# Down projection by seven block products instead of eight, in two passes over its weights

## The chip, the cores and the metric

The kernel runs on one core of a Trainium2 chip. TensorE (PE) multiplies matrices, VectorE (DVE), ScalarE (ACT) and GpSimd (POOL) work element by element, and SyncE's queue (SP) issues the DMAs. The metric is the device time of one execution in microseconds (us). Before the change the median of 3 runs is 704.86 us (703.7 to 706.74).

## What is computed

One decoder layer over 512 tokens of width 1024: a token mixer (differential attention and sparse attention), then a gated feed-forward part. The change lies in the last matrix product of the second:

```python
h = rms_norm(x, ffn_pre_norm[l])
f = (jax.nn.silu(h @ w_gate[l]) * (h @ w_up[l])) @ w_down[l]
x = x + rms_norm(f, ffn_post_norm[l])
```

`w_gate` and `w_up` are 1024 x 2816, `w_down` is 2816 x 1024, all in float32.

## The kernel before

**Three products for one.** TensorE reads float32 data rounded to the type fp32r. To keep the precision, every operand is cut into a high part (a rounded copy, made by ScalarE) and a low part (the operand minus the high part, made by VectorE), and a product is the sum of three: high by high, low by high, high by low. `split_w` (L142 for the high part, L152 for the low one) does this to a loaded weight tile of 128 x 1024.

**Feed-forward stage.** The 2816 features are 22 tiles (NF) of 128. For each tile f, `ff_gate` (L1045) issues 48 matmuls of 128x128 by 128x512: 24 for the gate and 24 for the up product, over 8 tiles of the model width (hth and htl, 128 x 8 x 512 each) and the three parts. Then the silu chain runs: an exponential on ScalarE (L1049), and on VectorE an addition (L1050), a reciprocal (L1051) and two multiplications (L1052, L1053), of which the first needs the gate product and the second the up product, both in PSUM. The result, features by tokens, is cut into `ffh` (L1054, ScalarE) and `ffl` (L1055, VectorE). The first two tiles are done in two halves of 256 tokens, since the norms of the last tokens are not ready yet.

**Down projection.** The output is 512 tokens by 1024 columns and fills all eight banks of PSUM, as four token tiles of 128 (i) by two column halves of 512 (c). `down` (L1083) issues three matmuls for one (i, c) and one feature tile f: a 128 x 128 block of ffh or ffl is the stationary operand, and half a row of the weight tile, 128 x 512, the moving one. That is 24 matmuls of a feature tile and 528 in all. For the first 19 tiles f is the outer loop; the last three (LAST) are taken with i outermost, so that the token tiles end one after the other and the closing norm of one lies beside the matmuls of the next. The closing work on a token tile: the squares on ScalarE (L983), the reciprocal root of their mean on ScalarE and VectorE in steps of one column (L161 to L170), the gain (L1099), the scaling and residual sum (L1101) on VectorE, and two DMAs out (L1102).

**Buffers and order.** Weight tiles go through three buffers each for the raw tile, the high and the low part; a raw buffer is free once the low part is made (L137 issues the load), and a high or low buffer once the matmuls that read it are done. 36 slots of 128 x 512 (`sslot`) and two tiles of four such (`rope_tile`) hold ffh and ffl. The instructions of this part stand in the program in the order in which a reader would write them, and a planner orders them on each engine by a timeline of its own: at each step the instruction that stands first in the program among those that are ready by its reckoning. On the chip the engines then keep this order.

Of the kernel before, what the change touches and what calls it, by code (L numbers as in the profile page):

```python
# [17 lines left out]
P = 128  # L18
# [84 lines left out]
LAST = 3  # L103
# [12 lines left out]
def hybrid_block_kernel(  # L116
# [843 lines left out]

    g_post, g_pre = gain(0), gain(1)
# [13 lines left out]
    def row_rsqrt(src, tag):  # L975
        ss = cpool.tile([P, 1], F32, tag="ss" + tag, name="ss", bufs=2)
        act.activation(junk[tag], src, AF.Square, accum_out=ss)
        return rsqrt_of(ss, tag)

    def halves_rsqrt(src, tag, also):  # L980
        ss = cpool.tile([P, 2], F32, tag="ss" + tag, name="ss", bufs=2)
        for c in range(2):
            act.activation(junk["a"][:, :SEQ], src[c], AF.Square, accum_out=ss[:, c:c + 1])  # L983
            if c == 0:
                also(c)
        dve.tensor_tensor(ss[:, 0:1], ss[:, 0:1], ss[:, 1:2], OP.add)
        r = rsqrt_of(ss[:, 0:1], tag)
        also(1)
        return r

    CS = [slice(c * SEQ, (c + 1) * SEQ) for c in range(2)]
# [14 lines left out]
    def norm_pre(i):  # L1006
# [4 lines left out]
        for c in range(2):  # L1011
# [4 lines left out]
            d_h, d_l = (t[:, 4 * c:4 * c + 4, i * P:(i + 1) * P] for t in (hth, htl))  # L1016
# [3 lines left out]
    ffh, ffl, ffw = [None] * NF, [None] * NF, []  # L1020

    def ff_alloc(f):
        for j, (l, n) in enumerate(((ffh, "ffh"), (ffl, "ffl"))):
            k = 2 * f + j
            if k < NS:
                l[f] = sslot(f"{n}{f}")
            else:
                k -= NS
                if k % 4 == 0:
                    ffw.append(rope_tile())  # L1030
                l[f] = ffw[-1][:, k % 4]
# [6 lines left out]
    def ff_gate(f, ws, s0, s1, tag):  # L1038
        pts = wide(tag, "gu")
        for wi, w in enumerate(ws):  # L1040
            pt = pts[wi][:, s0:s1]
            n = 0
            for ww, hx in ((w[0], hth), (w[0], htl), (w[1], hth)):
                for k in range(NK):
                    pe.matmul(pt, w_col(ww, k), hx[:, k, s0:s1],  # L1045
                              start=(n == 0), stop=(n == 3 * NK - 1))
                    n += 1
        sl = A.tile([P, SEQ], F32, tag="silu", name="silu", bufs=2)[:, s0:s1]
# [4 lines left out]
        dve.tensor_tensor(sl, sl, pts[1][:, s0:s1], OP.mult)  # L1053
        act.activation(ffh[f][:, s0:s1], sl, AF.Copy)  # L1054
        dve.tensor_tensor(ffl[f][:, s0:s1], sl, f32(ffh[f][:, s0:s1]), OP.subtract)  # L1055
# [18 lines left out]
    for f in range(2, NF):  # L1074
        ff_alloc(f)
        ff_gate(f, ff_weights(f), 0, SEQ, ("gu", "o", "tr", "o")[f % 4])

    g_ffn = gain(2)
    acc = [wide(t, "acc") for t in ("tr", "o", "gu", "o")]

    def down(i, f, w, first, last, c):
        for n, (a, wi) in enumerate(((ffh, 0), (ffl, 0), (ffh, 1))):
            pe.matmul(acc[i][c], a[f][:, i * P:(i + 1) * P],  # L1083
                      w[wi][:, c * SEQ:(c + 1) * SEQ],
                      start=(first and n == 0), stop=(last and n == 2))

    for f in range(NF - LAST):
        w = split_w(load_w(wd[f]))
        for i in range(NT):
            for c in range(2):  # L1090
                down(i, f, w, f == 0, False, c)
    ws = [split_w(load_w(wd[f])) for f in range(NF - LAST, NF)]
    for i in range(NT):
        for c in range(2):
            for n, w in enumerate(ws):
                down(i, NF - LAST + n, w, False, n == LAST - 1, c)
        u, a, x_ = work("uf"), acc[i], halves(x2[i])
        uh = halves(u)
        r = halves_rsqrt(a, "c", lambda c: dve.tensor_tensor(uh[c], a[c], g_ffn[:, CS[c]], OP.mult))  # L1099
# [94 lines left out]
```

## Time and profile before

| | us |
|---|---|
| median of 3 runs | 704.86 |
| the profiled execution | 707.53 |
| its span, first to last instruction | 705.8 |
| TensorE busy in the span | 677.2 (96%) |
| VectorE busy | 458.5 (65%) |
| ScalarE busy | 291.9 (41%) |
| mean granted TensorE clock | 0.983 of full speed |

Busy times are sums over the span; the stages differ, and so the rows further down are taken stage by stage. The page's own time in matmuls counts overlapping, since matmuls are pipelined: the distance from the start of one to the start of the next is what one costs.

### The profile page before, as it was taken

Reading aid. Unit: us, or ns where it says so; the run is one execution under the profiler, and the core shown is the slowest. Engines: PE = TensorE matmul, PEld = TensorE weight load, DVE = VectorE, ACT = ScalarE, POOL = GpSimd, SP = SyncE. Lnnn points to the kernel's source line nnn. Section 1 sums busy time; section 2 is a strip of 40 time slices with the busy share of each in tenths; the row PEclk is TensorE's granted clock in tenths of the full one; section 3 lists DMA queues with packets and bytes.
Section 4 is the critical chain, followed back from the end, with each engine's and each line's share of the span. In section 5 each row is a group of like instructions: output and inputs, shape, how many; then the busy total and the mean of one; then the engine's idle time right before and its main releaser. Section 6 shows DMA issues by size and latency. Waiting matters only on the chain.

```text
span 705.8 us, 9312 instructions
## 1 busy us (share of the span) xinstructions
PE 677.2 (96%) x3539; PEld 565.6 (80%) x3539; DVE 458.5 (65%) x712; ACT 291.9 (41%) x605; POOL 100.5 (14%) x151
## 2 busy tenths in 40 slices
PE   8999999989999999998799999999999999999995
PEld 4988778879787888777788888888888888888884
DVE  4787795856788574679676776867768672222227
ACT  7333352654787776534323233232332321211113
POOL 0000000028777934500000000000000000000000
PEclk9999999999999999999899999999999999999998
DMA  8357857623432030270022332223322332222303
GB/s 314 130 146 258 295 180 277 215 104 92 162 106 91 16 106 1 90 268 31 1 90 90 96 113 90 90 89 96 114 90 90 92 108 99 90 90 94 114 2 119
DMA packets 25980, 83.62 MB, mean 118 GB/s; under 512 B 3408, under 2 KB 4304, under 8 KB 25040
## 3 DMA queue, kind: packets, MB, share of 16 engines
q1 hardware_dynamic: 25936, 83.03, 35.2%
q8 instruction: 28, 0.46, 0.3%
q14 instruction: 16, 0.13, 0.1%
HBM read 73.06 MB, written 9.96 MB: 118 GB/s over the span
## 4 chain that ended last, share of the span: by engine, by line
PE 76%; DVE 10%; DMA 5%; issue 4%; ACT 3%; SPq 1%; POOL 0%; DVEq 0%; ACTq 0%; POOLq 0%
PE gu L1045 33%; PE acc L1083 16%; PE fm L327 8%; PE mixp L817 3%; PE v L413 3%; PE tr L574 3%; PE avn L754 2%; PE sc L548 2%; PE sc L549 2%; DMA qk<-rope 2%; DVE p L619 1%; DMA wraw<-in_wf 1%; DMA gain<-in_grow 1%; DMA wraw<-in_wvg 1%; PE av L631 1%
## 5 line engine op out<-in xcount | busy, mean ns | idle before, releaser
L152 DVE TENSOR_TENSOR wlo<-wraw,whi 128x1024 fp32r<-128x1024 f32 x86 | 104.9, 1222 | 142.1 <-ACT whi L142 97.5
L142 ACT ACTIVATE whi<-wraw 128x1024 fp32r<-128x1024 f32 x88 | 92.9, 1060 | 213.1 <-PE gu L1045 89.1
L1045 PE MATMUL gu<-hth,whi 128*128 128x512 f32 (+1 forms) x352 | 85.7, 386 | 0.5 <-ACT hth L1017 0.5
L1045 PE MATMUL gu<-htl,whi 128*128 128x512 f32 (+1 forms) x352 | 84.8, 384 | 0.0
L1045 PE MATMUL gu<-hth,wlo 128*128 128x512 f32 (+1 forms) x352 | 84.3, 382 | 0.0
L1045 PEld LDWEIGHTS gu<-hth,whi 128*128 128x128 f32 x352 | 65.4, 193 | 14.0 <-ACT hth L1017 0.8
L1045 PEld LDWEIGHTS gu<-htl,whi 128*128 128x128 f32 x352 | 64.9, 191 | 13.0
L1045 PEld LDWEIGHTS gu<-hth,wlo 128*128 128x128 f32 x352 | 64.1, 188 | 13.1
L1051 DVE RECIPROCAL silu<-silu 128x512 f32<-128x512 f32 (+1 forms) x24 | 74.1, 3086 | 0.7
L554 DVE TENSOR_REDUCE nm<-sc 128x1 f32<-128x384 f32 (+3 forms) x96 | 44.4, 484 | 21.7 <-PE sc L550 21.3
L1083 PE MATMUL acc<-whi,ffl 128*128 128x512 f32 x144 | 56.0, 389 | 0.0
L1083 PE MATMUL acc<-wlo,ffh 128*128 128x512 f32 x144 | 56.0, 389 | 0.0
L1083 PE MATMUL acc<-whi,ffh 128*128 128x512 f32 x144 | 55.9, 389 | 0.0
L558 ACT ACTIVATE p<-sc,nm 128x384 f32<-128x384 f32 (+3 forms) x96 | 50.0, 528 | 10.6 <-DVE nm L554 9.1
L723 POOL TENSOR_TENSOR p<-p,l 128x128 f32<-128x128 f32 (+2 forms) x64 | 45.6, 740 | 1.3
L587 DVE TENSOR_TENSOR ptl<-tr,pth 128x384 fp32r<-128x384 f32 (+1 forms) x60 | 35.1, 595 | 12.2 <-ACT pth L584 11.9
L548 PE MATMUL sc<-kst,qst 128*128 128x128 f32 (+1 forms) x96 | 36.2, 379 | 4.9 <-ACT p L558 3.2
L327 PE MATMUL fm<-xh,whi 128*128 128x512 f32 x128 | 34.4, 404 | 3.1 <-ACT whi L142 3.1
L584 ACT ACTIVATE pth<-tr 128x384 fp32r<-128x384 f32 (+1 forms) x60 | 31.0, 527 | 9.1 <-PE tr L574 8.3
L1054 ACT ACTIVATE ffh<-silu 128x512 fp32r<-128x512 f32 (+1 forms) x20 | 11.8, 589 | 52.4 <-DVE silu L1053 52.4
L327 PE MATMUL fm<-xh,wlo 128*128 128x512 f32 x128 | 32.4, 391 | 0.0
L327 PE MATMUL fm<-xl,whi 128*128 128x512 f32 x128 | 32.1, 390 | 0.0
(234 smaller groups left out, 1219.2 us busy)
## 6 DMA issues: line engine op xcount, KB each, us to landing
wraw<-in_wg SPq DMA_DIRECT2D x22, 512.0 KB, 3.3
wraw<-in_wu SPq DMA_DIRECT2D x22, 512.0 KB, 3.3
wraw<-in_wd SPq DMA_DIRECT2D x22, 512.0 KB, 3.3
wraw<-in_wf SPq DMA_DIRECT2D x16, 512.0 KB, 4.9
qk<-rope SPq DMA_DIRECT2D x7, 1024.0 KB, 4.7
kst<-qk SPq DMA_DIRECT2D x24, 256.0 KB, 3.6
qst<-qk SPq DMA_DIRECT2D x16, 256.0 KB, 2.7
wraw<-in_wo SPq DMA_DIRECT2D x8, 512.0 KB, 3.6
```

The source lines that it names most:

```text
L142: act.activation(dst, src, AF.Copy)
L152: (lo_eng or dve).tensor_tensor(lo[:, :w], raw[:, :w], f32(hi[:, :w]), OP.subtract)
L327: pe.matmul(pt, w[:, k * P:(k + 1) * P], xx[k], start=(n == 0), stop=(n == 3 * NK - 1))
L548: pe.matmul(sv[i], lhs, kk[:, 0, :w], start=True, stop=False)
L554: dve.tensor_reduce(nm[i], sv[i], AX.X, OP.max, negate=True)
L558: act.activation(pp[i], sv[i], AF.Exp, bias=nm[i], accum_out=hs["l"][:, row, i:i + 1])
L584: act.activation(part(u, 0), tv[u], AF.Copy)
L587: dve.tensor_tensor(part(u, 1), tv[u], f32(part(u, 0)), OP.subtract)
L723: pool.tensor_tensor(p, p, hs["l"][:, 1 + br, i:i + 1].to_broadcast(list(p.shape)), OP.mult)
L1045: pe.matmul(pt, w_col(ww, k), hx[:, k, s0:s1], start=(n == 0), stop=(n == 3 * NK - 1))
L1051: dve.reciprocal(sl, sl)
L1083: pe.matmul(acc[i][c], a[f][:, i * P:(i + 1) * P], w[wi][:, c * SEQ:(c + 1) * SEQ], start=(first and n == 0), stop=(last and n == 2))
```

## The change

Feature tiles are taken in pairs (2p, 2p+1) for p = 0 to 8. With tokens in two halves (256 each) and output columns in two halves (512 each), a pair's part of the output is a 2 x 2 by 2 x 2 product of blocks, and Winograd's form of Strassen's method makes it of seven block products, with sums of blocks on both sides made by VectorE. A block product is six matmuls of the shape used before: two token tiles by three parts. The last four feature tiles (18 to 21) go through `down` as before.

Since four results and the sums of products need more than eight banks, there are two passes. Pass A makes products 1, 5, 6 and 7 of all nine pairs in four accumulators of two banks. Products 1, 5 and 7 are then copied to SBUF, and `join` adds them up with product 6, still in PSUM, in pass B after pair 5. Pass B makes the other three products of each pair in the accumulators that have come free, and the last four tiles add to the same banks; the closing work adds PSUM to the parts in SBUF. Of the even weight tile the whole is loaded in pass A, of the odd one a half in pass A and the whole in pass B.

In the gate stage the cut of the 18 tiles into ffh and ffl is replaced by `pair_sums`, once a pair. The chain of the last tile (21) stands in the program behind the preparation of pairs 0 and 1. hth and htl become four tiles of 128 x 4 x 512, whose buffers are used again in the down projection.

```diff
-LAST = 3
+LAST = 4
+NPAIR = 9
+KEEP_R = (0, 1, 2, 3)
+HPV = 200
+JOIN = 5
...
-    hth = A.tile([P, NK, SEQ], F32R, name="hth")
-    htl = A.tile([P, NK, SEQ], F32R, name="htl")
-
-    junk = {t: A.tile([P, D_MODEL], BF16, name="junk" + t, bufs=1) for t in "ab"}
+    def quad(name):
+        return A.tile([P, 4, SEQ], F32R, tag="h", name=name, bufs=4)
+
+    hth, htl = ([quad(f"{n}{c}") for c in range(2)] for n in ("hth", "htl"))
+
+    junk = A.tile([P, SEQ], F32, name="junk", bufs=1)
...
-        act.activation(ffh[f][:, s0:s1], sl, AF.Copy)
-        dve.tensor_tensor(ffl[f][:, s0:s1], sl, f32(ffh[f][:, s0:s1]), OP.subtract)
+        p = f // 2
+        o = a2[p][:, s0:s1] if p < NPAIR and f % 2 else sl
+        dve.tensor_tensor(o, sl, pts[1][:, s0:s1], OP.mult)
+        if p >= NPAIR:
+            act.activation(ffh[f][:, s0:s1], sl, AF.Copy)
+            dve.tensor_tensor(ffl[f][:, s0:s1], sl, f32(ffh[f][:, s0:s1]), OP.subtract)
+        elif f % 2 and s1 == SEQ:
+            pair_sums(p)
+
+    def pair_sums(p):
...
+        act.activation(a11[p][:, LOW], x11, AF.Copy)
+        dve.tensor_tensor(s1, x21, x22, OP.add)
+        dve.tensor_tensor(s2, s1, x11, OP.subtract)
+        dve.tensor_tensor(s3, x11, x21, OP.subtract)
+        dve.tensor_tensor(s4, x12, s2, OP.subtract)
+        dve.tensor_tensor(a11[p][:, TOP], x11, f32(a11[p][:, LOW]), OP.subtract)
...
+    def cut(hi, lo, raw):
+        act.activation(hi, raw, AF.Copy)
+        dve.tensor_tensor(lo, raw, f32(hi), OP.subtract)
+
+    def product(acc, a, b, first, last):
+        for t in range(2):
+            for n, (x, y) in enumerate(((0, 0), (1, 0), (0, 1))):
+                pe.matmul(acc[t], a[x][:, t * P:(t + 1) * P], b[y],
+                          start=(first and n == 0), stop=(last and n == 2))
...
+    def prepare_a(p):
+        raw = load_w(wd[2 * p])
+        b22 = wpool.tile([P, 1024], F32, tag="raw", name="wraw", bufs=WB[0])
+        nc.sync.dma_start(b22[:, L], wd[2 * p + 1][:, H])
...
+        t3 = b22[:, H]
+        dve.tensor_tensor(t3, b22[:, L], raw[:, H], OP.subtract)
+        dve.tensor_tensor(raw[:, H], raw[:, H], raw[:, L], OP.subtract)
+        dve.tensor_tensor(t2[p], b22[:, L], raw[:, H], OP.subtract)
+        w = split_w(raw)
+        cut(th[:, L], tl[:, L], t2[p])
+        cut(th[:, H], tl[:, H], t3)
...
+        cut(h12, l12, s12[p])
+        cut(h3, l3, s34[p][:, LOW])
...
+    first2 = [prepare_a(p) for p in range(2)]
+    ff_chain(NF - 1, last_gate, 0, SEQ)
+    for names in ((1, 6, 5), (7,)):
+        for p in range(2):
+            products_a(p, first2[p], names)
+    for p in range(2, NPAIR - 2):
+        products_a(p, prepare_a(p), (1, 6, 5, 7))
+    last2 = {p: prepare_a(p) for p in (NPAIR - 2, NPAIR - 1)}
+    for n in (1, 5, 7, 6):
+        for p, ops in last2.items():
+            products_a(p, ops, (n,))
+    part = [[sslot(f"c{i}{c}", F32) for c in range(2)] for i in range(NT)]
+    for dst, acc in ((0, acc1), (1, acc5), (3, acc7)):
+        for i in range(2):
+            with tc.high_priority(offset=HPV):
+                act.activation(part[i + (dst & 2)][dst & 1], acc[i], AF.Copy)
+
+    def join():
+        for i in range(2):
+            (q11, q12), (q21, q22) = part[i], part[i + 2]
+            dve.tensor_tensor(q21, q11, acc6[i], OP.add)
+            dve.tensor_tensor(q12, q12, q21, OP.add)
+            dve.tensor_tensor(q21, q21, q22, OP.add)
+            dve.tensor_tensor(q22, q22, q12, OP.add)
+
+    def prepare_b(p):
+        raw = load_w(wd[2 * p + 1])
+        q, r = quad("tb"), sslot("s4")
+        dve.tensor_tensor(t2[p], raw[:, L], t2[p], OP.subtract)
+        w = split_w(raw)
+        cut(q[:, 0], q[:, 1], t2[p])
+        cut(q[:, 2], q[:, 3], a2[p])
+        cut(r[:, LOW], r[:, TOP], s34[p][:, TOP])
...
+    for p in range(NPAIR):
+        ops = prepare_b(p)
+        for n in (1, 5, 7):
+            product(accs[n], *ops[n], p == 0, False)
+        if p == JOIN:
+            join()
...
+    for i in (2, 3, 0, 1):
...
+        for c in (1, 0):
             for n, w in enumerate(ws):
-                down(i, NF - LAST + n, w, False, n == LAST - 1, c)
...
+                down(i, NF - LAST + n, w, n == LAST - 1, c)
+            a = part[i][c]
+            dve.tensor_tensor(a, a, quarter[i][c], OP.add)
+            act.activation(junk[:, :HS].bitcast(BF16), a, AF.Square, accum_out=ss[:, c:c + 1])
```

## Rows read from the trace of the kernel before

**Rows 1.** The chain of work that ended last, on the profile's page: shares of the span by engine.

```profile
PE 76%; DVE 10%; DMA 5%; issue 4%; ACT 3%; SPq 1%; POOL 0%; DVEq 0%; ACTq 0%; POOLq 0%
```

**Rows 2.** The view by stretches of time, for the feed-forward stage, the down projection and what lies behind its last matmul: start and end, length, busy time (and instructions) of PE, PE's weight loads, DVE, ACT and POOL, the granted TensorE clock, the DMA share and GB/s.

```profile
345.00:578.30 233.30, 233.30 (x1056) 193.89 (x1056) 166.74 (x151) 70.08 (x85) 0.00 (x0) 0.99 0.29 93
578.30:698.50 120.20, 119.96 (x530) 98.97 (x528) 35.05 (x50) 26.80 (x41) 0.00 (x0) 1.00 0.25 83
698.50:706.00 7.50, 0.00 (x0) 0.00 (x0) 3.97 (x10) 1.04 (x4) 0.00 (x0) 0.75 0.39 152
```

**Rows 3.** The view of groups by line, from 330 us to the end, the matmuls of the down projection (L1083): line, engine, operation, result and operands, shapes, count, busy us and mean ns of one, idle time before.

```profile
L1083 PE MATMUL acc<-whi,ffl 128*128 128x512 f32 x144 | 56.0, 389 | 0.0
...
L1083 PE MATMUL acc<-wlo,ffh 128*128 128x512 f32 x144 | 56.0, 389 | 0.0
...
L1083 PE MATMUL acc<-whi,ffh 128*128 128x512 f32 x144 | 55.9, 389 | 0.0
...
L1083 PE MATMUL acc<-whi,rope 128*128 128x512 f32 x64 | 19.2, 389 | 0.0
...
L1083 PE MATMUL acc<-wlo,rope 128*128 128x512 f32 x32 | 12.0, 389 | 0.0
```

**Rows 4.** The timeline of PE around the start and the end of the down projection, its first and its last matmul: start us, length us.

```profile
578.39 0.39 PE L1083 MATMUL acc<-whi,ffh 128*128 128x512 f32 x1
...
697.87 0.39 PE L1083 MATMUL acc<-wlo,rope 128*128 128x512 f32 x1
```

**Rows 5.** The view of groups by line with shapes kept apart, DVE from 330 us to the end: the subtraction or product of two operands at three sizes, in SBUF (L152, L1055) and with one operand in PSUM (L1099).

```profile
L152 DVE TENSOR_TENSOR wlo<-wraw,whi 128x1024 fp32r<-128x1024 f32 x61 | 74.6, 1222 | 129.7 <-ACT whi L142 85.1 <-PE gu L1045 44.6
...
L1055 DVE TENSOR_TENSOR ffl<-silu,ffh 128x512 fp32r<-128x512 f32 x16 | 11.1, 693 | 11.4 <-ACT ffh L1054 11.4
...
L1055 DVE TENSOR_TENSOR ffl<-silu,ffh 128x256 fp32r<-128x256 f32 x4 | 1.6, 408 | 1.0 <-ACT ffh L1054 1.0
...
L1099 DVE TENSOR_TENSOR uf<-acc,gain 128x512 f32<-128x512 f32 x8 | 5.5, 685 | 5.4 <-ACT junka L983 5.4
```

**Rows 6.** The timeline of DVE in the last two feature tiles of the gate stage and just behind it: start us, length us, line; in brackets the idle time before and what ended it.

```profile
563.77 3.35 DVE L1051 RECIPROCAL silu<-silu 128x512 f32<-128x512 f32 x1
567.16 0.69 DVE L1052 TENSOR_TENSOR silu<-silu,gu 128x512 f32<-128x512 f32 x1
567.76 1.22 DVE L152 TENSOR_TENSOR wlo<-wraw,whi 128x1024 fp32r<-128x1024 f32 x1
568.90 0.68 DVE L1053 TENSOR_TENSOR silu<-silu,gu 128x512 f32<-128x512 f32 x1
...
578.14 0.69 DVE L1052 TENSOR_TENSOR silu<-silu,gu 128x512 f32<-128x512 f32 x1
...
579.88 0.68 DVE L1053 TENSOR_TENSOR silu<-silu,gu 128x512 f32<-128x512 f32 x1
...
581.26 0.69 DVE L1055 TENSOR_TENSOR rope<-silu,rope 128x512 fp32r<-128x512 f32 x1 [0.70 <-ACT rope L1054]
```

**Rows 7.** The view by stretches, for the two last feature tiles of the gate stage (columns as in rows 2).

```profile
556.42:567.40 10.98, 10.98 (x49) 9.02 (x48) 8.02 (x8) 3.35 (x4) 0.00 (x0) 1.00 0.30 96
567.40:578.40 11.00, 11.00 (x50) 9.02 (x49) 8.04 (x8) 3.35 (x4) 0.00 (x0) 1.00 0.31 98
```

**Rows 8.** As rows 5, for ACT: rounded copies at three sizes.

```profile
L142 ACT ACTIVATE whi<-wraw 128x1024 fp32r<-128x1024 f32 x61 | 64.7, 1061 | 170.5 <-PE gu L1045 89.1 <-PE acc L1083 81.4
...
L1054 ACT ACTIVATE ffh<-silu 128x512 fp32r<-128x512 f32 x16 | 10.1, 632 | 44.2 <-DVE silu L1053 44.2
...
L1054 ACT ACTIVATE ffh<-silu 128x256 fp32r<-128x256 f32 x4 | 1.7, 417 | 8.1 <-DVE silu L1053 8.1
```

**Rows 9.** DMA: the view of issues (result and source, count, KB each, median us from issue to landing), then the last line of the view of the raw weight tiles in the down projection, and the row of the DMA queue's own waits for a raw buffer from 400 us on (us in total, times, longest).

```profile
wraw<-in_wd SPq DMA_DIRECT2D x22, 512.0 KB, 3.3
...
out<-uf SPq DMA_DIRECT2D x8, 256.0 KB, 2.0
...
DMA to landing us min/median/max: 3.1/3.3/3.9
...
SPq L137 <- DVE wlo L152: 169.2, 33, 7.9
```

**Rows 10.** The timeline of the end: the last token tile's squares, the sum of their two halves, the last scaling and the issue of the last DMAs.

```profile
698.36 0.60 ACT L983 ACTIVATE junka<-acc 128x512 bf16<-128x512 f32 x1 [1.41 <-PE acc L1083]
...
699.71 0.15 DVE L986 TENSOR_TENSOR ss<-ss 128x1 f32<-128x1 f32 x1
...
701.27 1.42 DVE L1101 SCALAR_TENSOR_TENSOR uf<-uf,rs,x 128x512 f32<-128x512 f32 x2
...
702.05 0.99 SPq L1102 DMA_DIRECT2D out<-uf  x2
```

**Rows 11.** The start of the feed-forward stage: three stretches (columns as in rows 2), the matmul behind the longest idle time of TensorE there, and a VectorE step that stands before it.

```profile
342.00:345.00 3.00, 1.78 (x10) 1.34 (x11) 2.46 (x5) 1.39 (x3) 0.00 (x0) 0.80 0.00 0
345.00:348.00 3.00, 3.00 (x16) 3.00 (x16) 0.77 (x2) 0.00 (x0) 0.00 (x0) 0.50 0.03 5
348.00:351.00 3.00, 3.00 (x18) 3.00 (x17) 0.00 (x0) 0.04 (x1) 0.00 (x0) 0.56 0.00 0
...
342.67 1.32 PE L1014 MATMUL trh<-ident,mixt 128*128 128x128 f32 x8 [3.90 <-DVE mixt L1009]
...
339.26 0.42 DVE L1055 TENSOR_TENSOR ffl<-silu,ffh 128x256 fp32r<-128x256 f32 x1
```

More of the change, by code (lines that the diff above doesn't have):

```diff
@@ L976, in row_rsqrt, with split_q @@
         ss = cpool.tile([P, 1], F32, tag="ss" + tag, name="ss", bufs=2)
-        act.activation(junk[tag], src, AF.Square, accum_out=ss)
+        act.activation(junk.bitcast(BF16), src, AF.Square, accum_out=ss)
         return rsqrt_of(ss, tag)
[L980 to L989, printed above, removed]
-    CS = [slice(c * SEQ, (c + 1) * SEQ) for c in range(2)]
+    CS = [slice(c * SEQ, (c + 1) * SEQ) for c in range(2)]
+    def split_q(raw):
+        q = quad("wq")
+        hi, lo = (q[:, 2 * j:2 * j + 2].rearrange("p a b -> p (a b)") for j in range(2))
+        to_r("a", hi, raw)
+        dve.tensor_tensor(lo, raw, f32(hi), OP.subtract)
+        return hi, lo
     def halves(t):
@@ L1015, in norm_pre, with kept @@
             tv = tr[c].rearrange("p (k t) -> p k t", t=P)
[L1016 removed]
+            d_h, d_l = (t[c][:, :, i * P:(i + 1) * P] for t in (hth, htl))
             act.activation(d_h, tv, AF.Copy)
             dve.tensor_tensor(d_l, tv, f32(d_h), OP.subtract)
[L1020 to L1031, printed above, removed]
+    ffw = []
+    def kept(name, j):
+        if j // 2 in KEEP_R:
+            j = 2 * KEEP_R.index(j // 2) + j % 2
+            if j % 4 == 0:
+                ffw.append(f32(rope_tile()))
+            return ffw[-1][:, j % 4]
+        return sslot(name, F32)
     def w_col(w, k):
@@ L1073, in hybrid_block_kernel @@
     ff_gate(1, w1, 256, SEQ, "o")
-    for f in range(2, NF):
+    GU = ("gu", "o", "tr", "o")
+    for f in range(2, NF - 1):
         ff_alloc(f)
-        ff_gate(f, ff_weights(f), 0, SEQ, ("gu", "o", "tr", "o")[f % 4])
+        ff_gate(f, ff_weights(f), 0, SEQ, GU[f % 4])
+    ff_alloc(NF - 1)
+    last_gate = ff_products(NF - 1, ff_weights(NF - 1), 0, SEQ, GU[(NF - 1) % 4])
     g_ffn = gain(2)
-    acc = [wide(t, "acc") for t in ("tr", "o", "gu", "o")]
-    def down(i, f, w, first, last, c):
+    acc1, acc6, acc5, acc7 = (wide(t, f"acc{n}") for n, t in ((1, "tr"), (6, "o"), (5, "gu"), (7, "o")))
@@ L1082, in down @@
+    def down(i, f, w, last, c):
+        first = f == 2 * NPAIR and c == 1 and i > 1
         for n, (a, wi) in enumerate(((ffh, 0), (ffl, 0), (ffh, 1))):
-            pe.matmul(acc[i][c], a[f][:, i * P:(i + 1) * P],
-                      w[wi][:, c * SEQ:(c + 1) * SEQ],
+            pe.matmul(quarter[i][c], a[f][:, i * P:(i + 1) * P], w[wi][:, CS[c]],
                       start=(first and n == 0), stop=(last and n == 2))
-    for f in range(NF - LAST):
+    quarter = [(acc1[i], acc5[i]) for i in range(2)] + [(acc7[i], acc6[i]) for i in range(2)]
@@ L1088, in hybrid_block_kernel @@
+    for p in range(NPAIR):
[4 more added lines that the diff above has]
+            join()
+    for f in range(2 * NPAIR, NF - LAST):
         w = split_w(load_w(wd[f]))
```

81 lines of the change are left out of this document (70 added, 11 removed).

## The prediction

> **What bounds the kernel now.** I read the profile from the end backwards. The chain of waits comes first: the reader is to see that TensorE holds 76% of it [rows 1]. Then the stretches of time: in the feed-forward stage and in the down projection TensorE is busy without a hole (233.30 of 233.30 us, 119.96 of 120.20) at a granted clock of 0.99 and 1.00, while VectorE has 35.05 and ScalarE 26.80 of the 120.20 us [rows 2]. So a matmul less in the down projection is time won, as long as the other two engines, which have little to do there, stay ahead of TensorE.
>
> The price of a matmul is not its busy time of 389 ns [rows 3], since they overlap. The five groups of rows 3 are 144 + 144 + 144 + 64 + 32 = 528 matmuls; the first starts at 578.39, the last at 697.87 [rows 4], so one costs 119.48 / 527 = 0.2267 us.
>
> **What goes.** A pair of feature tiles took 2 x 24 = 48 matmuls; seven products of six are 42. Nine pairs save 54, and 54 x 0.2267 = 12.24 us. The new matmuls have the old shape and the old order of the three parts.
>
> **What comes: VectorE's work.** Durations are 1.22 us for 1024 columns, 0.69 for 512, 0.41 for 256 [rows 5]. Two independent ones behind each other start closer: 567.16, 567.76, 568.90 [rows 6], that is 0.60 for 512 and 1.14 for 1024, so an instruction hides about 0.08 us in the next, and 0.33 is left for 256. One that needs its forerunner's result starts 0.04 after its end (563.77 + 3.35 to 567.16), so 0.73 for 512.
> A pair in pass A: three differences (0.60, 0.73, 0.73), the low part of the weights 1.14, three low parts of 512 (1.80), one of 256 (0.33): 5.33 us. With full durations, 6 x 0.69 + 1.22 + 0.41 = 5.77. I take the middle, 5.55, because some of the low parts will wait for ScalarE's copy, as the one at 581.26 did [rows 6]. TensorE needs 24 x 0.2267 = 5.44 us for the pair. So VectorE, idle for 70% of the stage before, is just as long as TensorE in pass A.
> A pair in pass B: 0.60 + 1.14 + 2 x 0.60 + 0.33 = 3.27 us against 18 x 0.2267 = 4.08.
> ScalarE's share is hidden: 1.06 + 3 x 0.63 + 0.42 = 3.37 us a pair in pass A [rows 8]. The six copies out of PSUM (about 0.6 each) are hidden too: the order 1, 5, 7, 6 of the last two pairs puts 36, 24 and 12 matmuls (8.2, 5.4 and 2.7 us) behind the accumulators concerned. If that cover went, pass B would start at most 1.2 us late.
>
> A rule of the Trainium skill speaks for the upper end: VectorE: DVE Perf Modes, section "The DRAIN you can't avoid", says that the next operation does not start until the pipeline has emptied. The trace agrees for dependent operations and disagrees for independent ones, by 0.08 us. By the rule alone a pair takes 5.77.
>
> **The race in pass A.** I set t = 0 where the gate stage's last matmul ends. VectorE is busy 8.02 + 8.04 of the last 21.98 us of that stage [rows 7], so 5.92 are free. Pairs 0 and 1 want 2 x 5.33, less their weights' low parts (1.14 each, which stand in rows 7 already, as the down projection's first two tiles) and less the lows of the sums that must wait for the buffers of hth and htl (0.93 each): 6.5. Backlog at t = 0: 0.6. Then come those four lows (1.9) and the rest of tile 21's chain, three operations after t = 0 as before (578.14, 579.88, 581.26 [rows 6], 2.1). Pair 2 starts at t = 4.6, pair 8 at 4.6 + 6 x 5.55 = 37.9. Its weights' low part is there after two differences, ScalarE's copy and the subtraction, 0.60 + 0.73 + 1.06 + 1.22 + 0.1 = 3.7: at 41.6. TensorE, unhindered, starts pair 7 at 7 x 5.44 = 38.1 and wants pair 8's weights six matmuls later, at 39.4, because the last two pairs are interleaved. **Stall 2.2 us.** With 5.33 it is 0.9, with 5.77 it is 3.5; below nothing it cannot be.
> Pairs 0 and 1 themselves cover tile 21's chain: the product that needs its banks (7) comes after 36 matmuls, 8.2 us, and the chain's last read of PSUM is 2.2 us behind the gate stage's end (579.88 + 0.68 against 578.39).
>
> **Pass B** has no stall. VectorE has 9 x 3.27 for the pairs, eight operations of 0.65 for the join and 4 x 1.14 for the last four tiles: 39.2 us. TensorE has 36.7 until the last stage, which asks for its four tiles over 2.0 us more; and VectorE is done with pass A some 6 us before TensorE, since some 24 matmuls stand behind the last preparation, and the buffers allow it to use that time for the next pairs.
>
> **Other edits.** In the gate stage a pair loses two low parts (1.2) and gains five operations of 256, two of them dependent (1.9): 16.06 becomes 16.8 of 21.98 us [rows 7], hidden. At the stage's start VectorE loses the low part at 339.26, which stands ahead of what TensorE waits 3.90 us for [rows 11]: 0.3 won. The clock fell behind that wait to 0.80, 0.50 and 0.56 in three stretches, which lost 1.78 x 0.20 + 3.00 x 0.50 + 3.00 x 0.44 = 3.2 us [rows 11]; between 0 and 3.2 more could be won if the shorter wait avoids it; I take 0.
> At the end the addition of PSUM to the part comes between the last matmul and the squares: one operation of 0.685 [rows 5] and a handover of 0.1, **+0.8**. Now the chain from the squares (698.36) to the last scaling's end (702.69) is 4.3 us, in which the sum of the two halves came only at 699.71 [rows 10]; bounds 0 (were that wait to go) and 1.5 (were another like it to come). A token tile gives VectorE 4 x 0.685 + 1.42 and some 0.8 in small steps, 5.0 us, against TensorE's 24 x 0.2267 = 5.4, so it keeps pace.
> The loads: a pair in pass A brings 768 KB instead of 1024. The half tile's load waits for a raw buffer, and behind it in SP's queue stand only later loads, as before, where that queue already waits for the low parts (169.2 us in total [rows 9]) while TensorE has no hole.
>
> **Sum.** -12.24 - 0.3 + 2.2 + 0.8 = -9.5 us. Against its own profiled execution, 707.53, that gives 698.0; this execution is 2.67 above the median 704.86, so the forecast for a median is **695.3**.
>
> **Rivals.**
> *VectorE at full durations* (5.77 a pair): for it, that a low part waits for a copy in rows 6; against it, the overlaps there. Stall 3.5, time 696.6.
> *The loop through the raw buffers.* There are three and a pair wants two. If the odd half of the next pair gets the buffer of the even tile, it waits for: a difference, a second one, ScalarE's copy, the low part, and its own load, and then the next pair's first difference waits for it: 0.69 + 0.73 + 1.06 + 1.22 + 0.2 = 3.9 us and a landing. 256 KB land in 2.0 us on the way out, 512 KB in 3.3 on the way in [rows 9]; with 2.4 the loop is 6.3 us. Then pair 8 starts at 42.4, its weights come at 46.1, stall 6.7: 699.8; at 6.6 a pair 701.6. Against it: the odd half's own buffer can come free sooner, after 0.69 + 0.63 + 0.7 + 0.69 + 0.2 = 2.9, which gives a loop of 5.3 and is covered. The Trainium skill, Perfetto Trace Analysis, section "Optimization Strategy", has the sign of it: the same gap repeating on the engine that should be full can mean too little room for the next tile. No row of the kernel before shows such a gap in this stage.
> *The same loop at its long end, slower than before.* If the half tile lands as late as a whole one (3.3 to 3.9 [rows 9]), the loop is 7.2 to 7.8 us and TensorE stands 1.8 to 2.4 us in each of six pairs. It decides from 39.4 + 11.7 = 4.6 + 6x + 3.7, that is x = 7.14. At 7.5 the stall is 13.9, the time 707.0, and with one fall of the clock (3.2) 710. For it: nothing in the trace has loads on the path of this stage, so nothing shows how they behave there; against it: half the bytes.
> *One long stall and the clock.* If the stalls fall together into one of about 4 us, as long as the 3.90 of rows 11, TensorE loses 3.2 more behind it: -12.24 - 0.3 + 4.0 + 0.8 + 3.2 = -4.5, time 700.3. Against it: the waits come pair by pair.
> *The matmuls do not get cheaper by their number*: if the operands in other buffers made one 0.235 instead of 0.2267, 474 of them would cost 3.9 more, 699.2. Against it: 389 ns in all five groups of rows 3, whatever the buffers.
>
> **How the numbers follow.** The forecast (692.3 without any stall or tail, to 698.5) has 0.47, full durations 0.15, the loop 0.16, the long loop 0.08, the clock 0.08, dearer matmuls 0.06. About 0.5% (3.5 us) is what can be told from no change: the limits are 701.3 and 708.4. Faster: 0.47 + 0.15 + 0.12 + 0.05 + 0.04 = 0.83; slower: 0.06 of the long loop; between: 0.11. The range runs from 691.5 (no stall, no tail, and a part of the clock's 3.2 at the stage's start) to 702 (the loop at 6.6); the long loop and part of the clock's case lie outside.
>
> **What would show it.** 474 matmuls at 0.227 from the gate stage's end, with some 2 us of idle time of TensorE, most of it before pair 8's weights, waiting for VectorE's low part; VectorE busy over 90% in pass A and 80% in pass B. Idle time of equal length at each pair, with VectorE itself waiting for a load, would show the loop. Squares that start 0.7 to 0.8 behind the last matmul show the tail. The prediction is wrong if TensorE's idle time in pass A is over 7 us, if the distance of matmuls has changed, or if the stages before the down projection have moved by more than 3 us.

## The result and the profile after

The changed kernel takes 698.99 us in the median of nine runs (696.23 to 701.49), the kernel before 706.26 in nine runs beside it (703.7 to 711.88): ratio 0.9896 [0.987, 0.9923], about 1% faster. The forecast was 695.3 (691.5 to 702). It stood on a median of three runs, 704.86, which came out 1.4 us higher over nine; against the profiled execution the forecast was 698.0, and the profiled one now took 698.99. The forecast gain was 9.5 us; the medians of nine runs give 7.3, the two profiled executions 8.5. So the size is roughly right. The terms behind it are not, and they were wrong in opposite directions.

The view by stretches of the changed kernel, columns as in [rows 2]: gate stage, projection up to the last matmul's end, the rest, and four pairs of pass A.

```profile
345.00:576.90 231.90, 231.90 (x1065) 192.46 (x1065) 178.15 (x187) 64.90 (x82) 0.00 (x0) 1.00 0.29 95
576.90:688.40 111.50, 110.23 (x475) 88.48 (x473) 94.26 (x155) 57.29 (x102) 0.00 (x0) 1.00 0.34 109
688.40:697.00 8.60, 0.00 (x0) 0.00 (x0) 4.74 (x11) 1.22 (x4) 0.00 (x0) 0.61 0.32 123
...
596.47:618.48 22.01, 22.01 (x97) 17.72 (x96) 20.13 (x30) 11.29 (x18) 0.00 (x0) 1.00 0.48 142
```

TensorE is still full, at a granted clock of 1.00 (its upper level, 2.4 GHz), and VectorE now works 94.26 of 111.50 us where it worked 35.05 of 120.20 [rows 2]. In the four pairs from 596.47 TensorE has no hole at all: the forecast stall of pass A is not there.

The timeline of PE: first matmul of the projection, its one large hole, last matmul.

```profile
576.92 0.63 PE L1129 MATMUL acc<-whi,a 128*128 128x512 f32 x2
...
629.36 0.73 PE L1129 MATMUL acc<-whi,tb 128*128 128x512 f32 x2 [1.07 <-ACT c L1196]
...
687.92 0.40 PE L1221 MATMUL acc<-wq,ffh 128*128 128x512 f32 x1
```

From the first to the last, 111.00 us against 119.48 [rows 4]. At the old distance 474 matmuls would take 473 x 0.2267 = 107.23. Where do the other 3.77 us sit? Four distances around 629.36 are 0.33 to 1.47 us long and hold 1.75 us more than usual (a fifth, 0.26, lies at 599.11); the remaining 2.0 are spread over all the others. Their mean is 0.2315 in pass A and 0.2305 behind it (start to start between 0.20 and 0.25 us, from the records of the trace). The groups by line show it too, in the mean duration of one:

```profile
L1129 PE MATMUL acc<-tt,sh 128*128 128x512 f32 x64 | 18.2, 394 | 0.0
...
L1221 PE MATMUL acc<-whi,ffh 128*128 128x512 f32 x24 | 9.4, 393 | 0.0
```

Before, every group had 389 [rows 3]. A few ns in this column look like nothing; 474 times they are a sixth of the 12.24 us.

| Term | Forecast | Measured |
|---|---|---|
| 54 matmuls fewer | -12.24 | -12.24 |
| a dearer matmul | 0 (rival: +3.9) | +2.0 |
| stall in pass A | +2.2 | 0 |
| start of pass B | 0 (at most 1.2) | +1.8, of which 1.07 idle |
| up to the first matmul of the projection | -0.3 | -1.5 (578.39 to 576.92) |
| from the last matmul's start to the end | +0.8 | +1.2 (7.89 to 9.12) |
| Sum | -9.5 | -8.7 (span 705.76 to 697.04) |

**Why pass A didn't stall.** The timeline of DVE, ACT and PE late in pass A: each pair's first difference, the rounded weights of pair 8, their low part, and the first matmuls that use the one and the other.

```profile
607.43 0.69 DVE L1152 TENSOR_TENSOR wraw<-wraw 128x512 f32<-128x512 f32 x1 [0.18 <-DMA wraw<-in_wd]
...
612.95 0.69 DVE L1152 TENSOR_TENSOR wraw<-wraw 128x512 f32<-128x512 f32 x1 [0.76 <-DMA wraw<-in_wd]
...
618.48 0.69 DVE L1152 TENSOR_TENSOR wraw<-wraw 128x512 f32<-128x512 f32 x1 [0.72 <-DMA wraw<-in_wd]
...
620.07 1.06 ACT L146 ACTIVATE whi<-wraw 128x1024 fp32r<-128x1024 f32 x1 [0.17 <-DVE wraw L1153]
...
621.38 1.08 PE L1129 MATMUL acc<-whi,a 128*128 128x512 f32 x4
621.75 1.22 DVE L156 TENSOR_TENSOR wlo<-wraw,whi 128x1024 fp32r<-128x1024 f32 x1
...
624.63 0.62 PE L1129 MATMUL acc<-wlo,a 128*128 128x512 f32 x2
```

VectorE begins a pair every 5.5 us and waits up to 0.76 for the half tile, whose issue in SP's queue waits for VectorE in turn: this is the loop through the raw buffers, at the short end that the prediction thought possible (5.3) and not at the 6.3 of its rival. TensorE's own pair is 24 x 0.2315 = 5.56, just longer. And the matmuls stand in another order than I assumed: the planner did not interleave the last two pairs, and it put those that need a low part 14 matmuls behind those that need only the high one (624.63 against 621.38). So the low part, ready at 622.97, is wanted at 624.63; the high part, ready at 621.13, is wanted at 621.38. The margin there is 0.25 us.

**Start of pass B.** The timeline of ACT, in the order of its queue:

```profile
625.74 0.58 ACT L1196 ACTIVATE c<-acc 128x512 f32<-128x512 f32 x1
...
627.76 1.06 ACT L146 ACTIVATE whi<-wraw 128x1024 fp32r<-128x1024 f32 x1 [1.45 <-DMA wraw<-in_wd]
...
628.73 1.56 ACT L1196 ACTIVATE c<-acc 128x512 f32<-128x512 f32 x3
```

A weight rounding of pass B waits 1.45 us for its load, and three copies out of PSUM stand behind it. The first of these frees the bank that TensorE wants.

**The end.** The timeline of DVE and ACT behind the last matmul:

```profile
688.36 0.69 DVE L1247 TENSOR_TENSOR c<-c,acc 128x512 f32<-128x512 f32 x1 [0.77 <-PE acc L1221]
688.96 1.41 DVE L1255 SCALAR_TENSOR_TENSOR uf<-uf,rs,x 128x512 f32<-128x512 f32 x2
689.14 0.63 ACT L1248 ACTIVATE junk<-c 128x512 bf16<-128x512 f32 x1 [2.04 <-DVE c L1247]
689.67 0.19 ACT L1248 ACTIVATION_READ_ACCUMULATOR junk<-c 128x1 f32 x1
690.29 0.69 DVE L1253 TENSOR_TENSOR uf<-c,gain 128x512 f32<-128x512 f32 x1
690.89 0.15 DVE L1251 TENSOR_TENSOR ss<-ss 128x1 f32<-128x1 f32 x1
```

The squares are done at 689.86, and their sum (L1251) comes 1.0 us later: VectorE's queue holds the two scalings of the token tile before, and the gain product, ahead of it.

### The profile page after: what moved, and what is told of

Same layout as the page of the kernel before. It is cut to its first block, busy times and chain, and to the rows that moved or that the text cites. A ratio compares the mean times of both kernels' runs of the same rounds, so it can differ in the third digit from the quotient of the medians.

```text
span 697.0 us, 9415 instructions
## 1 busy us (share of the span) xinstructions
PE 665.6 (95%) x3485; PEld 554.5 (80%) x3485; DVE 528.1 (76%) x852; ACT 317.6 (46%) x663; POOL 100.5 (14%) x151
## 4 chain that ended last, share of the span: by engine, by line
PE 73%; DVE 12%; DMA 6%; ACT 4%; issue 4%; POOL 0%; SPq 0%; DVEq 0%; ACTq 0%; POOLq 0%
PE gu L1059 35%; PE fm L331 8%; PE acc L1129 7%; PE mixp L821 3%; PE acc L1221 3%; PE v L417 3%; PE tr L578 3%; DMA wraw<-in_wd 2%; PE sc L552 2%; PE avn L758 2%; PE sc L553 2%; DMA wraw<-in_wf 1%; DVE p L623 1%; ACT whi L146 1%; DMA gain<-in_grow 1%
## 5 line engine op out<-in xcount | busy, mean ns | idle before, releaser
L552 PE MATMUL sc<-kst,qst 128*128 128x128 f32 (+1 forms) x96 | 36.7, 384 | 4.4 <-ACT p L562 3.2
L553 PE MATMUL sc<-kst,qst 128*128 128x128 f32 (+1 forms) x96 | 31.8, 331 | 0.0
L331 PEld LDWEIGHTS fm<-xh,whi 128*128 128x128 f32 x128 | 24.0, 191 | 9.7 <-ACT whi L146 4.7
L578 PE MATMUL tr<-ident,p 128*128 128x128 f32 x200 | 31.3, 277 | 0.2 <-DVE p L623 0.2
L331 PEld LDWEIGHTS fm<-xl,whi 128*128 128x128 f32 x128 | 23.8, 188 | 4.9
```

The lines of the kernel that those rows point to most:

```text
L331: pe.matmul(pt, w[:, k * P:(k + 1) * P], xx[k], start=(n == 0), stop=(n == 3 * NK - 1))
L552: pe.matmul(sv[i], lhs, kk[:, 0, :w], start=True, stop=False)
L553: pe.matmul(sv[i], lhs, kk[:, 1, :w], start=False, stop=False)
L578: pe.transpose(tr[:, n * P:(n + 1) * P], pp[i][:, j * P:(j + 1) * P], ident)
```

## The experiments

The question was what makes a matmul dearer. Two theories first: the work of VectorE and ScalarE beside the matmuls, or where the operands lie. Beside that, whether the hole and the tail are what the rows say.

**e1, the change again.** No edit.

> The changed kernel once more, unaltered, with a second profile. In its first profile a matmul of the two passes costs 0.231 to 0.233 us (0.2267 in the down projection of the kernel before), TensorE has one hole of 1.07 us where pass B begins, and 9.1 us lie between the start of the last matmul and the end. If the dearer matmul belongs to the kernel, the distance is 0.231 to 0.233 again; if it was a matter of that one execution, it is about 0.227 here. Time by both 696 to 701, 1.0% below the kernel before.

699.6 us in six runs, ratio 0.9912 [0.9887, 0.9938]. Distances 0.2314 and 0.2304, a hole of 0.67, the first matmul of the projection at 577.32. The dearer matmul and the hole belong to the kernel.

**e2, two repairs.**

```diff
-        w = split_w(raw)
+        if p == 2:
+            with tc.issue_after(copies[3].ins):
+                w = split_w(raw)
+        else:
+            w = split_w(raw)
...
-        dve.tensor_tensor(uh[0], a, g_ffn[:, CS[0]], OP.mult)
+        (pool if i == 1 else dve).tensor_tensor(uh[0], a, g_ffn[:, CS[0]], OP.mult)
```

> Two edits to the changed kernel: the rounding of pair 2's weights in pass B is queued behind four of the six copies out of PSUM on ScalarE, and the last token tile's second gain product goes to GpSimd. Theory (the copies stand behind a rounding that waits for a load): the hole of 1.07 us at the start of pass B is gone or under 0.3. Rival (the copies are late because ScalarE is simply full there): the hole stays near 1. Tail: from the last matmul's start to the end 8.4 to 8.6 instead of 9.1 if VectorE's queue was what held the last sum, 9.1 if not. Time 697 to 698 against 699 for the changed kernel beside it.

698.29 us in six runs, ratio 0.9881 [0.9855, 0.9908], not to be told from e1. With four copies ahead of the rounding the hole is gone, and the projection takes 109.26 us instead of 111.00: the 1.8 us are those copies. The tail grew to 9.60 us. The timeline of DVE and POOL at the end:

```profile
687.37 2.41 DVE L1260 SCALAR_TENSOR_TENSOR uf<-uf,rs,x 128x512 f32<-128x512 f32 x2
...
687.59 1.65 POOL L1258 TENSOR_TENSOR uf<-c,gain 128x512 f32<-128x512 f32 x1 [381.77 <-DVE c L1252]
...
689.71 0.15 DVE L1256 TENSOR_TENSOR ss<-ss 128x1 f32<-128x1 f32 x1
```

The same two scalings took 1.41 us before and take 2.41 beside GpSimd's product. The Trainium skill, SBUF — State Buffer, section "SBUF: two separate sides", says that a GpSimd operation and a VectorE operation with two operands in SBUF lock each other out for a whole instruction; the trace agrees, since the second scaling ends 0.54 us behind the GpSimd product. So the tail's half of e2 tests nothing: what the moved product freed, the lock took away.

**e3, VectorE's load taken away.** The low parts of both passes are left out, and other high parts are multiplied in their place (the result lacks these terms).

```diff
-        w = split_w(raw)
+        w = high_w(raw)
...
     def cut(hi, lo, raw):
         act.activation(hi, raw, AF.Copy)
-        dve.tensor_tensor(lo, raw, f32(hi), OP.subtract)
...
```

> The changed kernel without the low parts that VectorE makes in the two passes: the matmuls keep their number, shape and order, and in place of a low part each reads another high part, so the output is not the layer's. VectorE's work falls from 5.3 to about 2.1 us a pair in pass A and from 3.3 to 0.6 in pass B. Theory that work on the other engines beside a matmul makes it dearer: 0.227 to 0.229 us a matmul in both passes. Rival, that it is the place or order of the operands: 0.231 to 0.233 as before. If VectorE's pace held TensorE in pass A, pass A gets shorter by more than the matmul distance alone gives.

698.9 us in one run. The stretch of the projection (columns as in [rows 2]):

```profile
578.90:688.50 109.60, 109.60 (x475) 88.84 (x473) 45.16 (x78) 56.26 (x100) 0.00 (x0) 1.00 0.31 111
```

VectorE's 94 us are halved and the distance stays, 0.2313 in pass A and 0.2318 behind it; only the hole is gone. So VectorE does not pace the projection. That its load doesn't make the matmuls dear is not shown by this run alone, since other operands meet in it; e4 and e9 show it too.

**e4, load added to the kernel before.** Six subtractions and four copies a feature tile on operands that are not used further.

```diff
         w = split_w(load_w(wd[f]))
+        for k in range(6):
+            dve.tensor_tensor(sb[:, CS[k % 2]], sa[:, CS[0]], x2[k % 4][:, CS[k % 2]], OP.subtract)
...
```

> The kernel before with idle work added in its down projection: for each of the first 19 feature tiles six VectorE subtractions of 512 columns and four ScalarE copies of 512 columns between scratch tiles, on which nothing depends. VectorE then has about 4.9 and ScalarE 3.5 us a tile of 5.44 us, as in pass A. Theory that such work makes a matmul dearer: the distance rises from 0.2267 to 0.231 or more, and the projection of 528 matmuls by 2 to 3 us. Rival, place or order of operands: 0.2267 and no change.

710.35 us in one run, and not the test it was meant to be. Nothing tied the additions to their place, and the planner moved them ahead, into the gate stage, as the view of their line shows (count, duration, first and last start):

```profile
L1093 DVE TENSOR_TENSOR sb<-sa,x x114: 627/687/701, 338.9 to 540.2; 128x512 f32<-128x512 f32 x114
```

By accident it tests the gate stage: with VectorE busy 238.35 of 251.00 us there instead of 180.51 of 248.30, and ScalarE 117.56 instead of 76.84, the gate's distance is 0.2289 in both. The projection's, without any added load, is 0.2268.

**Where the operands lie.** The gate stage had a dearer matmul all along, 0.2289 in the kernel before (the mean of all distances from 360 to 570 us), with the same shape. The group by line, in the kernel before, has 391 ns where the projection has 389 [rows 3]:

```profile
L1045 PE MATMUL gu<-hth,whi 128*128 128x512 f32 x312 | 77.7, 391 | 0.0
```

What sets it apart? A tile has a start address in each partition of SBUF, the on-chip memory. In the compiled programs the weights' parts and the slots start at odd multiples of 64 bytes, the tiles of the FFN's right-hand pool (hth, htl, and after the change most block operands) at even ones. The old projection reads only the first kind, the gate one of each, and the change mixes them product by product. (The traces hold no addresses; that the two kinds differ by 64 bytes is borne out by what the shifts below do.) So: shift one pool by 64 bytes.

**e5 and e6, the right-hand pool shifted,** in the changed kernel and in the one before.

```diff
+    AP = ctx.enter_context(tc.tile_pool(name="apadp", bufs=1, side="right"))
+    AP.tile([P, 16], F32, name="apad")
     A = ctx.enter_context(tc.tile_pool(name="a", bufs=1, side="right", reuse_waits="tile"))
```

> The changed kernel with an idle tile of 64 bytes a partition opened ahead of the FFN's right-hand pool, so that all its tiles (the block operands of the products, the activations' quarters, the fourth weight pair of the last stage) move by 64 bytes; the order of TensorE's instructions is the same. Theory 'place': a matmul is dearest when one operand starts at an odd and the other at an even multiple of 64 bytes; the kernel before has both odd (0.2267 us), this shift makes both odd everywhere. It expects a mean distance of 0.227 us in both passes and the last stage (0.2316, 0.2304, 0.2300 before the shift), 0.227 in the gate and up products too (0.2288), a projection 2.2 us shorter (111.0 to 108.8) and a span some 4 us shorter: median near 695. Rival 'mixture': the distance grows because the two operands come from different pools, wherever they lie: distances, 111.0 and 699 stay. Rival 'bank or accumulator order': stays too.

> The kernel before with the same 64 bytes ahead of its FFN pool. Its projection takes both operands from the left-hand pools and must stay at 0.2267 us a matmul and 119.5 us. Its gate and up products take the moving operand from the shifted pool. Theory 'place': their distance falls from 0.2288 to 0.2267, over 1056 matmuls 2.2 us: ratio to the kernel before about 0.997. Rival 'mixture': 0.2288 stays, ratio 1.000.

e5: 694.15 us in six runs, ratio to the kernel before 0.984 [0.9803, 0.9878], which lies wholly below e1's. e6: 704.4 in twelve runs, 0.9979 [0.9955, 1.0002]. The groups by line, first e5 (gate, product, last stage), then e6 (gate):

```profile
L1061 PE MATMUL gu<-htl,whi 128*128 128x512 f32 x315 | 77.9, 389 | 0.0
...
L1131 PE MATMUL acc<-tt,sh 128*128 128x512 f32 x62 | 17.3, 389 | 0.0
...
L1223 PE MATMUL acc<-whi,ffh 128*128 128x512 f32 x24 | 9.3, 389 | 0.0
```

```profile
L1047 PE MATMUL gu<-htl,whi 128*128 128x512 f32 x312 | 77.1, 389 | 0.0
```

391 to 394 have become 389, and the distance is 0.2267 in the gate stage of both, 0.2272 and 0.2268 in the passes of e5. VectorE works 94.06 and ScalarE 57.25 us beside the projection of e5, as much as before the shift, so their load is not the cause; and TensorE's instructions stand in the same order, so neither a mixture of pools nor the order of banks is. e6's interval reaches 1.0002: its time alone would not show the gain, its distances do. The projection fell by less than expected, to 109.41: TensorE's pair, now 24 x 0.2272 = 5.45 us, is shorter than VectorE's 5.5, and pass A shows five distances of 0.25 to 0.36 us. The next bound has come up.

**e7, VectorE's work made longer,** one subtraction more a pair in pass A.

> The changed kernel with one more independent 128x512 subtraction on VectorE (0.60 us from start to start, result unused) at the end of the work of each of pairs 2 to 8 of pass A. Theory 'TensorE sets the pace in pass A': VectorE has 0.3 to 0.5 us a pair left (25.57 us of 27.52 busy), so pairs lengthen by at most 0.3 us and pass A by at most 1 us, all of it a wait for VectorE late in the pass. Rival 'VectorE and the raw buffers set the pace' (a pair every 5.4 to 5.5 us at either): each pair 0.5 to 0.6 longer, pass A 3 to 4 us longer.

696.79 us in one run. It fails as e4 did: the seven subtractions read tiles that are ready early and ran from 333.6 to 343.6 us.

**e8, the shift and both repairs,** with VectorE's queue in the last token tile made: two scalings, closing addition, sum of squares, gain product.

```diff
+            with tc.issue_after(scaled.ins) if (i, c) == (1, 0) else ExitStack():
+                dve.tensor_tensor(a, a, quarter[i][c], OP.add)
...
+        with tc.issue_after(s.ins) if i == 1 else ExitStack():
+            dve.tensor_tensor(uh[0], a, g_ffn[:, CS[0]], OP.mult)
...
```

> The 64 bytes, with the two repairs: four copies of finished accumulators ahead of the weight rounding of pass B's third pair in ScalarE's queue (hole of 0.7 to 1.1 us at the start of pass B), and in the last token tile the scalings of the tile before ahead of the closing addition and the sum of squares ahead of the second gain product, all on VectorE (last matmul to end 9.1 us, of which 1.1 is the squares' sum waiting in the queue). Theory 'place': 4 us from the shift, 0.9 from the hole, 0.8 to 1.2 from the tail: median 693.5 to 694.5. Rival 'mixture': only the repairs, 697.5 to 698.

695.27 us in six runs, 0.9825 [0.9788, 0.9861]. The projection takes 108.03 us, the tail still 9.1: the scalings held the addition back to 683.67, 1.19 us behind the last matmul's start instead of 0.43, and what was won behind it was lost ahead of it.

**e9 and e10, the kernel before with other addresses.** e9 shifts the slots (and the two `rope` tiles behind them) alone, so that stationary operands lie at even and moving ones at odd multiples; e10 shifts everything on the left, so that all operands lie at even ones.

```diff
+    SP = ctx.enter_context(tc.tile_pool(name="spadp", bufs=1, side="left"))
+    SP.tile([P, 16], F32, name="spad")
     S = ctx.enter_context(tc.tile_pool(name="s", bufs=NS, side="left"))
```

```diff
-    cpool.tile([P, 16], F32, name="cpad")
+    cpool.tile([P, 32], F32, name="cpad")
```

> The kernel before with 64 idle bytes a partition ahead of the left-hand pool of the slots alone: in the down projection the stationary operands (slots) now start at even multiples of 64 bytes, the moving ones (weights) stay at odd ones; nothing else of the projection changes. Theory 'place' (a matmul is dearer when its two operands differ in this): 0.2267 us rises to 0.231 to 0.236 everywhere, the projection from 119.5 to 122 to 124 us, in a kernel without any block products. Rival 'the block products or their pools make it': 0.2267 and 119.5 stay.

> The kernel before with 64 more idle bytes at the foot of the left-hand side, so that weights and slots both start at even multiples of 64 bytes, and in the gate and up products both operands as well. It tells two readings of 'place' apart. If operands only have to agree, projection and gate are at 0.2267. If what matters is that both are at odd multiples, the projection becomes dearer (0.229 to 0.236) and so does the gate.

One run each, 708.46 and 704.56 us (the kernel before 705.46 in eleven runs beside them). The groups of e9 and its first and last matmul of the projection, then those of e10 (projection, gate):

```profile
L1085 PE MATMUL acc<-whi,ffl 128*128 128x512 f32 x144 | 57.0, 396 | 0.0
L1085 PE MATMUL acc<-wlo,ffh 128*128 128x512 f32 x144 | 56.9, 395 | 0.0
...
576.04 0.39 PE L1085 MATMUL acc<-whi,ffh 128*128 128x512 f32 x1
...
699.01 0.40 PE L1085 MATMUL acc<-wlo,rope 128*128 128x512 f32 x1
```

```profile
L1083 PE MATMUL acc<-wlo,ffh 128*128 128x512 f32 x144 | 56.0, 389 | 0.0
...
L1045 PE MATMUL gu<-hth,wlo 128*128 128x512 f32 x312 | 77.1, 389 | 0.0
```

In e9 (699.01 - 576.04) / 527 = 0.2333: 3.5 us more for the same 528 matmuls, in a kernel without block products and with VectorE busy only 34.70 of 123.00 us. In e10 all is at 389. So it is not the odd multiple: the two operands have to agree.

Mean distances and lengths of all kernels that bear on it, from the records (us; S stationary, M moving; the gate from 360 to 570 us):

| Kernel | Gate | Projection | First to last |
|---|---|---|---|
| before | 0.2289 (S odd, M even) | 0.2267 (both odd) | 119.48 |
| e9 | 0.2289 (S odd, M even) | 0.2333 (S even, M odd) | 122.97 |
| e6 | 0.2267 (both odd) | 0.2267 (both odd) | 119.45 |
| e10 | 0.2267 (both even) | 0.2267 (both even) | 119.45 |
| after | 0.2289 (S odd, M even) | 0.2315, 0.2305 (mixed) | 111.00 |
| e5 | 0.2267 (both odd) | 0.2272, 0.2268 (both odd) | 109.41 |

**e11, e7 mended:** the additional operation reads the pair's own parts (and its result is not used).

```diff
         cut(h3, l3, s34[p][:, LOW])
+        if p > 1:
+            dve.tensor_tensor(junk, f32(th[:, H]), f32(tl[:, H]), OP.add)
```

> As e7, with the additional subtraction made an addition that reads the pair's own T3 parts, so that it can't be queued before its pair: seven more of 0.60 us on VectorE during pass A, junk in the result. Theory 'TensorE sets the pace of pass A and VectorE has 0.4 us a pair to spare': pass A from 50.0 to at most 51.5 us. Rival 'VectorE with the raw buffers sets it': 53 to 54 us.

700.64 us in one run; pass A takes 50.79 us instead of 50.03. The timeline of DVE, the first differences of four pairs:

```profile
599.15 0.69 DVE L1152 TENSOR_TENSOR wraw<-wraw 128x512 f32<-128x512 f32 x1
...
605.03 0.68 DVE L1152 TENSOR_TENSOR wraw<-wraw 128x512 f32<-128x512 f32 x1
...
610.90 0.68 DVE L1152 TENSOR_TENSOR wraw<-wraw 128x512 f32<-128x512 f32 x1
616.38 0.69 DVE L1152 TENSOR_TENSOR wraw<-wraw 128x512 f32<-128x512 f32 x1
```

Seven times 0.60 us (the last at 625.14, behind all that pass A needs) cost 0.76. Pairs of VectorE go from 5.5 to 5.9 us for a while and TensorE draws on its lead. TensorE paces pass A of the changed kernel, and VectorE has less than half a microsecond a pair to spare.

**e12, the shift and both repairs, mended:** in the last token tile first scaling, closing addition, second scaling, sum of squares, a step of the root, gain product.

```diff
...
+            with tc.issue_after(sc.ins) if (i, c) == (1, 0) else ExitStack():
+                v = dve.tensor_tensor(a, a, quarter[i][c], OP.add)
+            if (i, c) == (1, 0):
+                with tc.issue_after(v.ins):
+                    scale_out(0, 1, *held)
...
+        with tc.issue_after(marks[-1].ins) if i == 1 else ExitStack():
+            dve.tensor_tensor(uh[0], a, g_ffn[:, CS[0]], OP.mult)
```

> The shift of 64 bytes, the four copies ahead of the weight rounding, and in the last token tile VectorE's queue in the order: first scaling of the tile before, closing addition, second scaling, sum of squares, second gain product. Against e8, whose two scalings stood together ahead of the addition and held it back by 0.85 us: squares' sum 0.8 us earlier, last matmul to end 8.4 instead of 9.2 us, projection 108.0 us as there. Span 690.8, median about 694 (e8 695.27, e5 694.15).

694.67 us in six runs, 0.9849 [0.9824, 0.9873]. The timeline of DVE and PE at the end:

```profile
683.77 0.39 PE L1230 MATMUL acc<-wq,ffh 128*128 128x512 f32 x1
...
684.30 0.68 DVE L1263 TENSOR_TENSOR c<-c,acc 128x512 f32<-128x512 f32 x1
684.90 0.74 DVE L1250 SCALAR_TENSOR_TENSOR uf<-uf,rs,x 128x512 f32<-128x512 f32 x1
...
685.83 0.16 DVE L1270 TENSOR_TENSOR ss<-ss 128x1 f32<-128x1 f32 x1 [0.19 <-ACT junk L1267]
```

The sum of squares comes 2.06 us behind the last matmul's start instead of 2.97, the end 8.4 instead of 9.1, and the projection takes 108.11 us. The median is not below e5's all the same: in this profile the projection began at 575.67, in e5's at 572.99, behind stages that both kernels have in common. The two can't be told apart, nor from e8. All three are faster than the kernel before, and than the change as it stood in e1 (e12's upper end 0.9873, e1's lower one 0.9887; in the first nine runs of the change the lower end was 0.987, so that this step is a narrow one in time).

## Why the prediction came out as it did

The removal was right to the matmul: 474 matmuls, 12.24 us at the old price. TensorE does set the time. That the sum came within 0.8 us of the forecast is luck in part: a stall of 2.2 us that did not come stands against dearer matmuls and a late pass B, 3.8 us together, which the sum had at nothing, and the start won 1.2 us more than forecast for a reason that no run shows.

**"The new matmuls have the old shape", and so the old price** is the step that failed. Shape and order are the same, the place is not. The rival that held it, "the matmuls do not get cheaper by their number", was given 0.235 and a chance of 0.06; measured were 0.2315 and 0.2305, 2.0 us. The argument against it was "389 ns in all five groups of rows 3, whatever the buffers". But all those buffers lie alike. The counterexample stood in the same trace: the gate stage's matmuls of the same shape, at 0.2289 a piece. I never worked out their distance, since the gate stage wasn't changed. By the prediction's own list a changed distance makes it wrong, and to that extent it is.

**The stall of 2.2 us** failed in its order, not in its engine. VectorE was later than forecast: pair 8 begins 41.6 us behind the gate stage's end, forecast 37.9. The delay arose ahead of pair 4, which begins at 19.6 instead of 15.7 (VectorE worked 17.2 of these 19.6 us and waited 1.76 for one copy of ScalarE); from there on pairs follow at 5.5 as forecast. TensorE wanted its low part much later (47.7, forecast 39.4), because the last two pairs were not interleaved and the low parts come last in each pair. I took the order from the program's text, though a planner makes it. The price of a pair, 5.55 us of VectorE's time, was 5.03 (20.13 / 4): the planner puts other operations between those that depend on each other. The rest of the 5.5 is mostly waiting for the half tile. The Trainium skill's rule (VectorE: DVE Perf Modes, section "The DRAIN you can't avoid"), 5.77 by the prediction's reckoning, is further off; the section itself adds that a next operation that is not held starts earlier, which the prediction left out and [rows 6] show.

**The copies, "at most 1.2 us late"**, cost 1.8. The bound counted matmuls behind the accumulators as cover and forgot what stands ahead of the copies in their own queue: a weight rounding that waits for a load. e2 shows it by moving that one instruction.

**The tail** has the right mechanism, an addition between matmul and squares, +0.8: the squares start 1.22 us behind the last matmul's start instead of 0.49. A queue of VectorE adds to it, total 1.2. The bound of 1.5 was for "another like it", and this is what it was. e12 takes 0.76 of it back.

**The start** is open. The forecast had TensorE's wait there 0.3 us shorter; it grew from 3.90 to 4.89. It is now at 328.26 instead of 342.67, and behind it the clock falls to half, the lower level (1.2 GHz), as before [rows 11]:

```profile
328.26 1.86 PE L1018 MATMUL trh<-ident,mixt 128*128 128x128 f32 x8 [4.89 <-DVE mixt L1013]
...
331.00:334.00 3.00, 3.00 (x15) 3.00 (x15) 3.00 (x10) 0.70 (x5) 0.00 (x0) 0.50 0.48 179
```

Whether the change won the 1.5 us can't be said: e9, with the old code in these stages, reached the projection at 576.04, 2.35 us sooner than the profile of before, and e1 to e3, with the change's code in them, at 577.07 to 578.92.

**The rivals.** The raw-buffer loop runs at 5.5 us, hidden behind TensorE by 0.06; e5 lays it bare. Its long end was never near: the half tile landed in 2.7 us. The stall with a falling clock did not come; the hole of 1.07 left the granted clock at 1.00.

## What to carry to other kernels

Before you price a new instruction by an old one of its shape, ask where the operands of both lie, and look in the same trace for a group of that shape with another distance. Here two tiles that TensorE reads together were cheapest when they started alike modulo 128 bytes: 64 idle bytes were worth some 3.7 us (2.1 in the gate stage, 1.6 in the projection), nearly a third of what 54 matmuls brought. Whether another kernel gains by it, a shift of 64 bytes will tell. Where a planner orders the queues, read the order it made before you reckon a race, and tie an experiment's added work to its place by its data.

## What the runs showed of the hardware that was not expected

A 128x128 by 128x512 matmul of fp32r data with a weight load of its own takes 0.2267 us from start to start when both operands start at odd or both at even multiples of 64 bytes in their partition. It takes 0.2289 with the stationary one odd and the moving one even (gate stage), and 0.2333 with the two the other way round (projection of e9). The two stages also differ in how often they change the accumulator, so that the direction alone makes the difference is not shown. These are means of a pattern that repeats: 0.226, 0.229 and 0.232 in the gate stage, 0.231 and 0.236 in e9, where agreeing operands have 0.226 or 0.227 throughout. The load on VectorE does not matter (e4, e5, e9). Where neighbours in the queue differ, as after the change, the distance scatters from 0.224 to 0.237, also for matmuls whose own operands agree: product 6 has both in the right-hand pool, and where both its neighbours are its own kind it still takes 0.2320, against 0.2266 in e5. What a matmul owes to those ahead of it was not taken apart. Other shifts than 64 bytes, other types and other shapes were not tried, and which part of the chip makes it was not shown.
